# Stick-breaking attention: the scores of a head pair made in one go, in turns on two row groups and into two PSUM banks

## The chip, the cores and the metric

One NeuronCore of a Trainium2 chip runs the whole program; the other cores are idle. The metric is the device time of one execution in microseconds (us). TensorE (PE) does the matrix products, ScalarE (ACT) and VectorE (DVE) the elementwise work and the reading of PSUM, GpSimd (POOL) a few memsets and small operations, and SyncE (SP) issues the transfers. Each engine works through its own list of instructions strictly in the order in which the program was built.

## What is computed

A block of a streaming encoder over 528 tokens of width 1024: a feed-forward layer, a mixer with two kinds of attention, and a second feed-forward layer. The part that the change touches is the stick-breaking attention with 8 heads of width 64:

```
z = einsum('bhtd,bhsd->bhts', q, k) * scale
strict = s < t
log_1m = where(strict, log_sigmoid(-z), 0)
csum = cumsum(log_1m, axis=-1)
log_a = log_sigmoid(z) + csum[..., -1:] - csum
a = where(strict, exp(log_a), 0)
out = einsum('bhts,bhsd->bhtd', a, v)
```

So each score needs the sum of `log_1m` over all later keys. The kernel gets that sum as a product with a triangular matrix, key block by key block from the last to the first, and carries the sum of the later blocks in one row.

## The kernel before, in words

All float32 operands are split into a high and a low part (`split`: one cast and one subtraction), and a product is three matmuls: high by high, high by low, low by high (`mm3`).

The mixer's second part works on four **pairs** of heads, p = 0 to 3. For a pair, `sb_qk` makes the keys `KS` and queries `QS`: head 0 lies on partitions 0 to 63 of these tiles, head 1 on partitions 64 to 127. `sb_attn` then goes over five key blocks i = 4 to 0, which have 20, 146, 274, 400 and 512 query columns, and calls `sb_tile` for head 0 and then for head 1. One call of `sb_tile` is this chain, in which every link needs the one before it:

1. three score matmuls with 64 contraction rows into one PSUM tile `z` (line 1146);
2. DVE adds the mask (1150); ACT takes Abs, Exp and Ln (1154 to 1156); DVE adds max(z, 0) (1157), casts the result to `shi` (196) and subtracts for `slo` (197);
3. row 0 of `shi` and `slo` gets the carry, which is read from row 0 of the `z` tile of the previous key block of the same head (ACT 1164, DVE 1165);
4. two matmuls with the triangular matrix `tri` add the suffix sums onto `z` (1170 for `shi`, 1172 for `slo`);
5. ACT takes Exp (1175) and casts (192), DVE subtracts (197);
6. two matmuls with V add to the head's output `ysb` (1110, 1111). After the last block `out_v` copies and adds (1115, 1116).

A `z` tile is a whole PSUM bank; there are four of them (`bufs=4`), so two heads and two key blocks fill them. A head's `z` of one block is free once the carry of its next block has been read.

Between the steps of this chain PE works on other products, the **fillers**: `fillers()` makes the next pair's `QS` and `KS` (tiles pk, pq), the latents of the other attention (pc, pkr), the gates (`gt`, 24 matmuls of 512 columns for each), and the first parts of the latent attention (muqr, muqs, muk, muq, muv). How many of these are handed out between two tiles is set by `FILL_RATE`. The order of instructions on each engine is not written by hand: a scheduler builds it from the program, the priorities (`ATT_PRIO` for the stick-breaking tiles) and its own estimate of durations. Behind the fourth pair come the output projection `osb` (which needs all four pairs) and the latent attention (sc, pt, ymla).

Of the kernel before, what the change touches and what calls it, by code (L numbers as in the profile page):

```python
# [9 lines left out]
F32 = mybir.dt.float32  # L10
F32R = mybir.dt.float32r
AF = mybir.ActivationFunctionType
ALU = mybir.AluOpType
# [24 lines left out]
CST = [0, 112, 238, 366, 492]  # L38
KROWS = [128, 128, 128, 128, 21]
# [18 lines left out]
ATT_PRIO = 3000  # L58
# [25 lines left out]
class Block:  # L84
# [1033 lines left out]
    def sb_attn(self, qk, V, p):  # L1118
        yo = []
        prev = [None, None]  # L1120
        for i in range(4, -1, -1):
            for heads in ((0,), (1,)):
                with self.tc.high_priority(ATT_PRIO):
                    self.sb_tile(qk, V, p, i, heads, prev, yo)
                yield i == 0 and heads == (1,)
        with self.tc.high_priority(ATT_PRIO):
            t = self.M(f"ysb{p}")
            for h in range(2):
                self.out_v(t[64 * h:64 * h + 64, :512], yo[h], True)
        self.ysb = t  # L1130

    def sb_tile(self, qk, V, p, i, heads, prev, yo):
        nc, tc = self.nc, self.tc
        KS, QS = qk
        m, c0 = KROWS[i], CST[i]
        n = 512 - c0
        nh = len(heads)

        def three(t):
            return t[:m, :nh * n].rearrange("p (h c) -> p h c", h=nh)  # L1140
        pv = three(self.z("z"))
        for x, h in enumerate(heads):
            r = slice(64 * h, 64 * h + 64)
            kc = slice(128 * i, 128 * i + m)
            for t, (kx, qx) in enumerate(((0, 0), (0, 1), (1, 0))):
                nc.tensor.matmul(pv[:, x], KS[r, kx, kc], QS[r, qx, c0:512], start=x == 0 and t == 0, stop=False,
                                 skip_group_check=True)
        mw = MASKW[i]
        msl = self.ms[:m, SHIFT[i]:SHIFT[i] + mw]
        nc.vector.tensor_tensor(pv[:, :, :mw], pv[:, :, :mw],  # L1150
                                msl.unsqueeze(1).to_broadcast([m, nh, mw]), ALU.add)
        ev, hi, lo = three(self.E("e", F32)), three(self.E("shi")), three(self.E("slo"))
        with tc.issue_after(self.pre):
            nc.scalar.activation(ev, pv, AF.Abs)
            nc.scalar.activation(ev, ev, AF.Exp, scale=-1.0)
            nc.scalar.activation(ev, ev, AF.Ln, bias=1.0)
        nc.vector.scalar_tensor_tensor(ev, pv, 0.0, ev, ALU.max, ALU.add)
        self.split(hi, lo, ev, "dve")
        d = n
        if prev[heads[0]] is not None:  # L1160
            d = CST[i + 1] - c0
            pps, x = prev[heads[0]]
            src = pps[0:1, x:x + 1]
            nc.scalar.mul(hi[0:1, :, d:n], src, -1.0)
            nc.vector.scalar_tensor_tensor(lo[0:1, :, d:n], src, -1.0, hi[0:1, :, d:n].bitcast(F32),
                                           ALU.mult, ALU.subtract)
        nc.gpsimd.memset(hi[0:1, :, :d].bitcast(F32), 0.0)
        nc.gpsimd.memset(lo[0:1, :, :d].bitcast(F32), 0.0)
        for x in range(nh):
            nc.tensor.matmul(pv[:, x], self.tri[:m, :m], hi[:, x], start=False, stop=False,  # L1170
                             skip_group_check=True)
            nc.tensor.matmul(pv[:, x], self.tri[:m, :m], lo[:, x], start=False, stop=True,
                             skip_group_check=True)
        with tc.issue_after(self.pre):
            nc.scalar.activation(ev, pv, AF.Exp)
        self.split(hi, lo, ev, "act")
        if not yo:
            yo += [self.y("ysb") for _ in range(2)]
        for x, h in enumerate(heads):
            self.mm_v(yo[h], V[i], 2 * p + h, m, c0, hi[:, x], lo[:, x], i == 4, i == 0)  # L1180
            prev[h] = (pv, x)

    def mla_latents(self, a):

# [344 lines left out]
```

## Time and profile before

| | us |
|---|---|
| median of 3 runs (1213.14 to 1215.94) | 1213.72 |
| the profiled execution | 1213.73 |
| its span, first to last instruction | 1211.6 |
| PE busy in it | 1179.5 (97%) |
| ACT, DVE busy in it | 634.8, 833.1 |
| stick-breaking attention, first score to last V product | 431.7 to 672 |

The page gives busy times and the chain of work that ended last; the time line gives single instructions with their start and how long each took. Matmuls follow each other closely, so the pitch (start to start) says what a matmul costs, and its own duration is longer than that. A row of the time line with x3 stands for three instructions in a row; its second number is the time from the first start to the last end. What stands in brackets at the end of a row is how long the engine was idle before it and what ended the wait.

### The profile page before, as it was taken

What the parts mean: (1) busy time and instruction counts of PE and PEld (TensorE: products, weight loads), DVE (VectorE), ACT (ScalarE), POOL (GpSimd) and SP (SyncE); (2) the same over time, 40 slices, a digit from 0 to 9 for tenths busy, and PEclk for the clock granted to TensorE, in tenths of its full rate; (3) what the DMA queues carried; (4) which work ended last, traced back from release to release, by engine and by line L of the source; (5) the groups of instructions that cost most, each with busy time, mean ns of one, the idle gap of its engine ahead of it and who ended that gap; (6) DMA issues with size and microseconds to landing.
All of it is one profiled execution on the core that took longest, in us unless ns stands there. A gap on an engine that the chain in (4) does not pass through costs nothing.

```text
span 1211.6 us, 20678 instructions
## 1 busy us (share of the span) xinstructions
PE 1179.5 (97%) x7928; PEld 1067.2 (88%) x7928; DVE 833.1 (69%) x1628; ACT 634.8 (52%) x1353; POOL 114.4 (9%) x189
## 2 busy tenths in 40 slices
PE   8999999999999999999999999999999999999997
PEld 8999999999999977878876777768988999889987
DVE  7754886579778655655576667489785588458945
ACT  6544564245554446555666657556364466226632
POOL 0000000000000011110020333360000000000004
PEclk9999999999998999999999999999999999999999
DMA  6233234223431421223232135353144223313441
GB/s 217 71 101 91 90 104 140 71 87 98 166 122 55 149 96 62 88 87 106 83 106 84 62 101 178 103 185 123 36 161 154 70 90 125 118 54 105 148 148 70
DMA packets 46594, 130.29 MB, mean 108 GB/s; under 512 B 5368, under 2 KB 8824, under 8 KB 46496
## 3 DMA queue, kind: packets, MB, share of 16 engines
q1 hardware_dynamic: 46208, 128.88, 32.7%
q8 instruction: 62, 1.02, 0.3%
q14 instruction: 36, 0.29, 0.1%
q10 hardware_dynamic: 288, 0.10, 0.0%
HBM read 114.99 MB, written 12.58 MB: 105 GB/s over the span
## 4 chain that ended last, share of the span: by engine, by line
PE 86%; DVE 6%; ACT 3%; issue 2%; DMA 2%; POOL 1%; SPq 0%; DVEq 0%; ACTq 0%; POOLq 0%
PE pg L169 5%; PE pu L171 5%; PE pg L171 5%; PE pu L170 5%; PE pu L169 5%; PE pg L170 5%; PE down L732 3%; PE down L734 3%; PE down L733 3%; PE down L169 2%; PE down L171 2%; PE down L170 2%; PE gt L169 2%; PE gt L171 2%; PE gt L170 2%
## 5 line engine op out<-in xcount | busy, mean ns | idle before, releaser
L192 ACT CAST wp<-ws 128x512 fp32r<-128x512 f32 x144 | 87.1, 621 | 88.2 <-DVE ws L507 51.9
L197 DVE TENSOR_TENSOR wp<-ws,wp 128x512 fp32r<-128x512 f32 x144 | 97.0, 688 | 27.7 <-ACT wp L192 26.9
L197 DVE TENSOR_TENSOR wdl<-wdr,wdh 128x1024 fp32r<-128x1024 f32 (+1 forms) x42 | 49.2, 1172 | 42.7 <-ACT wdh L192 26.5
L192 ACT CAST wdh<-wdr 128x1024 fp32r<-128x1024 f32 (+1 forms) x42 | 42.4, 1009 | 56.4 <-PE pu L171 18.5
L169 PE MATMUL pu<-un,wp 128*128 128x264 f32 (+1 forms) x216 | 60.7, 283 | 0.0
L170 PE MATMUL pu<-un,wp 128*128 128x264 f32 (+1 forms) x216 | 60.7, 281 | 0.0
L170 PE MATMUL pg<-un,wp 128*128 128x264 f32 (+1 forms) x216 | 60.6, 282 | 0.0
L169 PE MATMUL pg<-un,wp 128*128 128x264 f32 (+1 forms) x216 | 60.5, 282 | 0.0
L171 PE MATMUL pu<-un,wp 128*128 128x264 f32 (+1 forms) x216 | 60.3, 282 | 0.0
L171 PE MATMUL pg<-un,wp 128*128 128x264 f32 (+1 forms) x216 | 60.2, 282 | 0.0
L169 PE MATMUL down<-g,wdh 128*128 128x272 f32 (+1 forms) x208 | 59.4, 290 | 0.4 <-ACT wdh L192 0.4
L170 PE MATMUL down<-g,wdh 128*128 128x272 f32 (+1 forms) x208 | 59.0, 287 | 0.0
L171 PE MATMUL down<-g,wdl 128*128 128x272 f32 (+1 forms) x208 | 58.8, 287 | 0.0
L733 PE MATMUL down<-wdl,g 128*128 128x512 f32 x144 | 56.8, 394 | 0.0
L734 PE MATMUL down<-wdh,g 128*128 128x512 f32 x144 | 56.1, 394 | 0.0
L732 PE MATMUL down<-wdh,g 128*128 128x512 f32 x144 | 55.1, 395 | 0.0
L169 PE MATMUL pg<-mcd,wp 128*128 128x264 f32 (+1 forms) x144 | 41.0, 285 | 1.7 <-ACT kept L497 1.7
L192 ACT CAST wp<-wpr 128x512 fp32r<-128x512 f32 x54 | 32.1, 621 | 18.9 <-DMA wpr<-g1p 11.2
L171 PE MATMUL pu<-mab,wp 128*128 128x264 f32 (+1 forms) x144 | 40.9, 284 | 0.0
L171 PE MATMUL pg<-mcd,wp 128*128 128x264 f32 (+1 forms) x144 | 40.9, 284 | 0.0
L170 PE MATMUL pg<-mcd,wp 128*128 128x264 f32 (+1 forms) x144 | 40.8, 283 | 0.0
L170 PE MATMUL pu<-mab,wp 128*128 128x264 f32 (+1 forms) x144 | 40.8, 283 | 0.0
(470 smaller groups left out, 4337.2 us busy)
## 6 DMA issues: line engine op xcount, KB each, us to landing
wdr<-d SPq DMA_DIRECT2D x38, 512.0 KB, 3.6
wpx<-u1p SPq DMA_DIRECT2D x18, 512.0 KB
wpr<-g1p SPq DMA_DIRECT2D x18, 512.0 KB, 3.7
wpx<-u2p SPq DMA_DIRECT2D x18, 512.0 KB, 4.7
wpr<-g2p SPq DMA_DIRECT2D x18, 512.0 KB, 3.8
wgtr<-w_in SPq DMA_DIRECT2D x16, 512.0 KB, 3.5
wxr<-w_out SPq DMA_DIRECT2D x8, 512.0 KB, 4.2
gl<-gates SPq DMA_DIRECT2D x16, 256.0 KB, 4.5
```

What stands on the lines that cost most here:

```text
L169: mm(out, wh, xh, start=first, stop=False, skip_group_check=True)
L170: mm(out, wh, xl, start=False, stop=False, skip_group_check=True)
L171: return mm(out, wl, xh, start=False, stop=last, skip_group_check=True).ins
L192: self.cast = nc.scalar.copy(hi, src).ins
L197: return nc.vector.tensor_tensor(lo, src, hi.bitcast(F32), ALU.subtract).ins
L732: mm(o, gt[:, 0, s], wh, start=fi == 0, stop=False, skip_group_check=True)
L733: mm(o, gt[:, 0, s], wl, start=False, stop=False, skip_group_check=True)
L734: mm(o, gt[:, 1, s], wh, start=False, stop=fi == nf - 1, skip_group_check=True)
```

## The change

The three score matmuls of a head leave `sb_tile`. A new function `sb_scores` takes two `z` tiles at once and issues the six score matmuls of both heads in turns: head 0, head 1, head 0, and so on, each ordered behind the one before it (`after(last)`). So neighbours read from partitions 0 to 63 and 64 to 127 and write to different banks. `sb_attn` calls it once per key block, and then `sb_tile` for each head with the tile that it is handed. The generality of `sb_tile` over several heads in one tile goes away with it; each tile still does the same elementwise work.

```diff
         for i in range(4, -1, -1):
-            for heads in ((0,), (1,)):
+            with self.tc.high_priority(ATT_PRIO):
+                pv = self.sb_scores(qk, i)
+            for h in range(2):
                 with self.tc.high_priority(ATT_PRIO):
-                    self.sb_tile(qk, V, p, i, heads, prev, yo)
-                yield i == 0 and heads == (1,)
+                    self.sb_tile(V, p, i, h, pv[h], prev, yo)
+                yield i == 0 and h == 1
...
+    def sb_scores(self, qk, i):
+
         KS, QS = qk
         m, c0 = KROWS[i], CST[i]
+        pv = [self.z("z")[:m, :512 - c0] for _ in range(2)]
+        kc = slice(128 * i, 128 * i + m)
+        last = None
+        for t, (kx, qx) in enumerate(((0, 0), (0, 1), (1, 0))):
+            for h in range(2):
+                r = slice(64 * h, 64 * h + 64)
+                with self.after(last):
+                    last = self.nc.tensor.matmul(pv[h], KS[r, kx, kc], QS[r, qx, c0:512], start=t == 0, stop=False,
+                                                 skip_group_check=True).ins
+        return pv
...
-        for x, h in enumerate(heads):
-            r = slice(64 * h, 64 * h + 64)
-            kc = slice(128 * i, 128 * i + m)
-            for t, (kx, qx) in enumerate(((0, 0), (0, 1), (1, 0))):
-                nc.tensor.matmul(pv[:, x], KS[r, kx, kc], QS[r, qx, c0:512], start=x == 0 and t == 0, stop=False,
-                                 skip_group_check=True)
```

The scheduler builds a new order from this. Three places show what it does. The names: z is a score tile, pv, gt, muk, muqr, muqs and muv are fillers, ysb are the products with V.

PE, first pair, the scores of 274 columns: two neighbouring pieces of the difference from before (-) to after (+).

```order
-L1170 MATMUL z<-shi,tri 128x146
-L1172 MATMUL z<-slo,tri 128x146
-L1146 MATMUL z<-QS_5158,KS_5094 128x274 x3
+L1172 MATMUL z<-shi,tri 128x146
+L1173 MATMUL z<-slo,tri 128x146
+L1145 MATMUL z<-QS_5158,KS_5094 128x274
 L170 MATMUL pv<-wvl,u_4552 128x512
 L171 MATMUL pv<-wvh,u_4552 128x512
```

```order
-L1170 MATMUL z<-shi,tri 128x146
-L1172 MATMUL z<-slo,tri 128x146
-L1146 MATMUL z<-QS_5158,KS_5094 128x274 x3
 L170 MATMUL pv<-wvl,u_4546 128x512
 L171 MATMUL pv<-wvh,u_4546 128x512
+L1172 MATMUL z<-shi,tri 128x146
+L1173 MATMUL z<-slo,tri 128x146
+L1145 MATMUL z<-QS_5158,KS_5094 128x274 x5
```

Two groups of three became a group of one (head 0 alone, as soon as its bank is free) and a group of five (once head 1's bank is free too); both heads' scores are whole at the end of the five.

PE, end of the third pair (p = 2): what follows the last scores, those of 512 columns. First before, from the products with `tri` of head 0 on:

```order
L1170 MATMUL z<-shi,tri 128x512
L169 MATMUL muqr<-ch,wuqrh 128x512
L1172 MATMUL z<-slo,tri 128x512
L1146 MATMUL z<-QS_6687,KS_6623 21x20 x3
L170 MATMUL muqr<-cl,wuqrh 128x512
L171 MATMUL muqr<-ch,wuqrl 128x512
L169 MATMUL muqs<-ch,wuqrh 128x512
L170 MATMUL muqs<-cl,wuqrh 128x512
L171 MATMUL muqs<-ch,wuqrl 128x512
L169 MATMUL muqs<-ch,wuqrh 128x512
```

And after, from the last products with V of 400 columns on:

```order
L1110 MATMUL ysb<-shi,V_5278 128x400
L1111 MATMUL ysb<-slo,V_5278 64x400
L1172 MATMUL z<-shi,tri 128x512
L1173 MATMUL z<-slo,tri 128x512
L1145 MATMUL z<-QS_6687,KS_6623 21x20 x6
L1110 MATMUL ysb<-shi,V_5246 128x512
L1172 MATMUL z<-shi,tri 128x512
L1111 MATMUL ysb<-slo,V_5246 64x512
L1173 MATMUL z<-slo,tri 128x512
L1145 MATMUL z<-QS_6687,KS_6623 128x146
L1172 MATMUL z<-shi,tri 21x20
L1173 MATMUL z<-slo,tri 21x20
```

Before, 59 fillers of 512 columns stand between head 1's scores and the pair's last product with V of 512 columns; after, only 8 fillers of 264 columns (muk) do, and the gate that filled the place stands behind them all. The ACT order at this place after the change, from head 0's Abs on:

```order
L1158 ACTIVATE e<-z 128x512
L192 CAST KM_7191<-muk 64x264
L1159 ACTIVATE e<-e 128x512
L1160 ACTIVATE e<-e 128x512
L1158 ACTIVATE e<-z 128x512
L1159 ACTIVATE e<-e 128x512
L1167 ACTIVATE shi<-z 1x400
L1160 ACTIVATE e<-e 128x512
L1175 ACTIVATE e<-z 128x512
L192 CAST shi<-e 128x512
L1167 ACTIVATE shi<-z 1x400
```

Abs, Exp and Ln of the two heads now stand one behind the other, since both heads' scores come at the same time.

PE, end of the fourth pair: what follows the last scores. Before, with head 1's last scores at the top:

```order
L1146 MATMUL z<-QS_6687,KS_6623 128x512 x3
L1172 MATMUL z<-slo,tri 128x400
L169 MATMUL muv<-wuvh,ch 16x512
L170 MATMUL muv<-wuvl,ch 16x512
L171 MATMUL muv<-wuvh,cl 16x512
L169 MATMUL gt<-u_4552,wgth 128x512
L1110 MATMUL ysb<-shi,V_5278 128x400
L170 MATMUL gt<-u_4552,wgth 128x512
L171 MATMUL gt<-u_4552,wgtl 128x512
L1111 MATMUL ysb<-slo,V_5278 64x400
```

After, with the group of five at the top:

```order
L1145 MATMUL z<-QS_6687,KS_6623 128x512 x5
L1173 MATMUL z<-slo,tri 128x400
L1111 MATMUL ysb<-slo,V_5278 64x400
L169 MATMUL muv<-wuvh,ch 128x512
L170 MATMUL muv<-wuvl,ch 128x512
L171 MATMUL muv<-wuvh,cl 128x512
L169 MATMUL muv<-wuvh,ch 128x512
L170 MATMUL muv<-wuvl,ch 128x512
L171 MATMUL muv<-wuvh,cl 128x512
L1110 MATMUL ysb<-shi,V_5278 128x400
L1111 MATMUL ysb<-slo,V_5278 64x400
L1172 MATMUL z<-shi,tri 128x512
```

From the last scores to the last product with V, 30 fillers of 512 columns (27 muv, 3 gt) stand before and 6 after; the 12 sc matmuls of the latent attention stand there in both. Over all four pairs, PE's runs of score matmuls with nothing else between them number 36 before and 39 after.

## Rows read from the trace of the kernel before

**Rows 1.** The page: the chain that ended last, by engine.

```profile
PE 86%; DVE 6%; ACT 3%; issue 2%; DMA 2%; POOL 1%; SPq 0%; DVEq 0%; ACTq 0%; POOLq 0%
```

**Rows 2.** Stretches: start:end, length, busy us (x instructions) of PE, PEld, DVE, ACT, POOL, clock, DMA.

```profile
600.00:625.00 25.00, 25.00 (x114) 18.52 (x113) 17.27 (x38) 16.33 (x37) 3.87 (x14) 1.00 0.33 111
...
650.00:675.00 25.00, 21.47 (x86) 15.15 (x84) 17.37 (x35) 18.07 (x38) 0.83 (x5) 0.93 0.26 74
...
700.00:800.00 100.00, 90.72 (x468) 69.92 (x466) 68.24 (x146) 65.39 (x153) 40.85 (x33) 0.98 0.43 144
```

**Rows 3.** Time line of PE: start, length, line, shape, count [idle before]. Scores among others.

```profile
474.90 0.49 PE L1146 MATMUL z<-QS,KS 64*128 64x512 f32 x1
475.33 0.34 PE L1111 MATMUL ysb<-slo,V 128*64 128x274 f32 x1
...
651.39 0.34 PE L1172 MATMUL z<-slo,tri 128*128 128x400 f32 x1
651.67 0.96 PE L1146 MATMUL z<-QS,KS 64*128 64x512 f32 x3
652.56 0.49 PE L171 MATMUL gt<-u,wgtl 128*128 128x512 f32 x1
652.89 0.39 PE L169 MATMUL gt<-u,wgth 128*128 128x512 f32 x1
653.12 0.40 PE L170 MATMUL gt<-u,wgth 128*128 128x512 f32 x1
```

**Rows 4.** Time line of PE: the two score matmuls in flight at 431.93.

```profile
431.78 0.31 PE L1146 MATMUL z<-QS,KS 64*128 64x146 f32 x2
```

**Rows 5.** Time line of PE: third pair, 512 columns, both heads' scores and last V product.

```profile
602.12 0.96 PE L1146 MATMUL z<-QS,KS 64*128 64x512 f32 x3
...
606.38 0.95 PE L1146 MATMUL z<-QS,KS 64*128 64x512 f32 x3
...
621.42 0.39 PE L1111 MATMUL ysb<-slo,V 128*64 128x512 f32 x1
```

**Rows 6.** Time line of ACT: links of the chain at 512 columns, fourth pair.

```profile
653.03 0.60 ACT L1154 ACTIVATE e<-z 128x512 f32<-128x512 f32 x1
...
654.32 0.63 ACT L1156 ACTIVATE e<-e 128x512 f32<-128x512 f32 x1
...
660.34 0.49 ACT L1164 ACTIVATE shi<-z 1x400 fp32r<-1x400 f32 x1
...
669.61 0.60 ACT L1175 ACTIVATE e<-z 128x512 f32<-128x512 f32 x1
670.30 0.62 ACT L192 CAST shi<-e 128x512 fp32r<-128x512 f32 x1
```

**Rows 7.** Time line of DVE: links of the chain at 512 columns, fourth pair.

```profile
654.98 0.69 DVE L1157 SCALAR_TENSOR_TENSOR e<-z,e 128x512 f32<-128x512 f32 x1 [1.42 <-ACT e L1156]
...
657.13 0.41 DVE L196 CAST shi<-e 128x512 fp32r<-128x512 f32 x1
...
661.61 0.56 DVE L1165 SCALAR_TENSOR_TENSOR slo<-z,shi 1x400 fp32r<-1x400 f32 x1
...
670.95 0.69 DVE L197 TENSOR_TENSOR slo<-e,shi 128x512 fp32r<-128x512 f32 x1 [0.79 <-ACT shi L192]
```

**Rows 8.** Time line of PE: end of the fourth pair.

```profile
656.83 0.45 PE L1172 MATMUL z<-slo,tri 128*128 128x400 f32 x1
...
660.97 0.47 PE L1170 MATMUL z<-shi,tri 128*128 128x512 f32 x1 [1.19 <-ACT shi L1164]
...
669.14 0.40 PE L1172 MATMUL z<-slo,tri 128*128 128x512 f32 x1
...
671.80 0.40 PE L1111 MATMUL ysb<-slo,V 128*64 128x512 f32 x1
```

**Rows 9.** Stretches, columns as in rows 2: just after that wait, and the whole end.

```profile
656.83:671.80 14.97, 13.60 (x56) 10.33 (x55) 10.40 (x21) 10.59 (x22) 0.63 (x4) 0.89 0.23 64
...
661.63:665.04 3.41, 3.41 (x11) 2.73 (x11) 2.15 (x6) 1.25 (x4) 0.00 (x0) 0.50 0.62 192
```

More of the change, by code (lines that the diff above doesn't have):

```diff
@@ L1130, in sb_attn, with sb_tile @@
         self.ysb = t
-    def sb_tile(self, qk, V, p, i, heads, prev, yo):
-        nc, tc = self.nc, self.tc
+    def sb_scores(self, qk, i):
         KS, QS = qk
         m, c0 = KROWS[i], CST[i]
-        n = 512 - c0
[L1137 to L1141, printed above, removed]
-        for x, h in enumerate(heads):
-            r = slice(64 * h, 64 * h + 64)
-            kc = slice(128 * i, 128 * i + m)
-            for t, (kx, qx) in enumerate(((0, 0), (0, 1), (1, 0))):
-                nc.tensor.matmul(pv[:, x], KS[r, kx, kc], QS[r, qx, c0:512], start=x == 0 and t == 0, stop=False,
-                                 skip_group_check=True)
+        pv = [self.z("z")[:m, :512 - c0] for _ in range(2)]
[8 more added lines that the diff above has]
+        return pv
+    def sb_tile(self, V, p, i, h, pv, prev, yo):
+        nc, tc = self.nc, self.tc
+        m, c0 = KROWS[i], CST[i]
+        n = 512 - c0
         mw = MASKW[i]
         msl = self.ms[:m, SHIFT[i]:SHIFT[i] + mw]
-        nc.vector.tensor_tensor(pv[:, :, :mw], pv[:, :, :mw],
-                                msl.unsqueeze(1).to_broadcast([m, nh, mw]), ALU.add)
-        ev, hi, lo = three(self.E("e", F32)), three(self.E("shi")), three(self.E("slo"))
+        nc.vector.tensor_tensor(pv[:, :mw], pv[:, :mw], msl, ALU.add)
+        ev, hi, lo = (t[:m, :n] for t in (self.E("e", F32), self.E("shi"), self.E("slo")))
         with tc.issue_after(self.pre):
@@ L1159, in sb_tile @@
         d = n
-        if prev[heads[0]] is not None:
+        if prev[h] is not None:
             d = CST[i + 1] - c0
[L1162 to L1165, printed above, removed]
+            src = prev[h][0:1]
+            nc.scalar.mul(hi[0:1, d:n], src, -1.0)
+            nc.vector.scalar_tensor_tensor(lo[0:1, d:n], src, -1.0, hi[0:1, d:n].bitcast(F32),
                                            ALU.mult, ALU.subtract)
[L1167 to L1173, printed above, removed]
+        nc.gpsimd.memset(hi[0:1, :d].bitcast(F32), 0.0)
+        nc.gpsimd.memset(lo[0:1, :d].bitcast(F32), 0.0)
+        nc.tensor.matmul(pv, self.tri[:m, :m], hi, start=False, stop=False, skip_group_check=True)
+        nc.tensor.matmul(pv, self.tri[:m, :m], lo, start=False, stop=True, skip_group_check=True)
         with tc.issue_after(self.pre):
@@ L1178, in sb_tile @@
             yo += [self.y("ysb") for _ in range(2)]
-        for x, h in enumerate(heads):
-            self.mm_v(yo[h], V[i], 2 * p + h, m, c0, hi[:, x], lo[:, x], i == 4, i == 0)
-            prev[h] = (pv, x)
+        self.mm_v(yo[h], V[i], 2 * p + h, m, c0, hi, lo, i == 4, i == 0)
+        prev[h] = pv
     def mla_latents(self, a):
```

## Prediction

> **What bounds the kernel now.** I read the chain that ended last first: TensorE holds 86% of it [rows 1]. So what counts is PE's work plus the time PE stands idle, stage by stage. Then the table of stretches: from 600 to 625 us, in the middle of the attention that is changed, PE is busy for all of 25.00 us, while ACT and DVE have room (16.33 and 17.27). From 650 to 675, where the fourth pair ends, PE is busy for 21.47 only, and from 700 to 800, in the latent attention, for 90.72 of 100 [rows 2]. So the stick-breaking stage is bound by PE's list as long as the list offers other work between the links of the attention chain. Saved PE time is then gained in full; a place where the list offers nothing is lost in full, since PE takes its instructions in order.
>
> **Part 1, the score matmuls.** The time line prices them by the pitch of starts. A gate matmul of 512 columns costs 0.23 (652.89 to 653.12). The triple of one head at 512 columns runs from 651.67 to 652.56, 0.89; with 0.28 ahead of it (0.18 would do for 400 columns) and 0.33 behind it (0.23 would do), a visit to the 64-row matmuls costs 0.10 + 0.20 + 0.10 = 0.40 over its columns. A single score matmul takes 0.43, 474.90 to 475.33 [rows 3].
>
> In a group of five, head 1's first stands beside head 0's second, and so on: three slots if neighbours on different rows run side by side. The trace holds such a case: in the first pair the scheduler happened to put two heads in turns, and two matmuls of 146 columns are in flight together, both within 0.31 [rows 4]; one behind the other, even at the pitch of a gate by columns, the second would start 0.07 later. At 146 columns a slot may be set by something other than the columns, so the row doesn't fix the gain at 512; I take the slots in full by it, and keep zero for the range. The Trainium skill (TensorE: Matmul & The Clock Gate, Part 3: Packing small matmuls) says that matmuls on different row groups run at the same time, starting about 4 ns apart, also at 512 columns; by it the slots come out in full.
>
> Before, a pair of triples has six slots; after, a group of one and a group of five have four. Two slots saved are 0.89 - 0.43 = 0.46 at 512 columns, by columns 0.36 at 400, 0.25 at 274 and 0.13 at 146. The first three occur in four pairs (4 x 1.07 = 4.28), the last in three, since the first pair's was in turns already (0.39): 4.7 us.
>
> Against it, the number of visits doesn't fall: because a group waits for head 1's bank, one visit of six became two, and some are cut further, 36 before and 39 after. Three more at 0.40 are 1.2. The Trainium skill (TensorEngine Tiling (Array Packing), Key Properties) says that changing the tiling mode drains the engine, which speaks against a change that cuts its groups; the 0.40 of the row agrees, and without that price the saving would be 4.7. **Saved on PE: 4.7 - 1.2 = 3.5 us** (bounds: +4.7 and -1.2).
>
> **Part 2, the third pair's end.** Both heads' scores are now whole at the same moment, so two chains run in step through ACT and DVE, and the scheduler put almost nothing between their links: 8 muk of 264 columns where 59 fillers of 512 stood. Before, both heads' scores of 512 columns ran at 602.12 and 606.38 and the last V product at 621.42, with PE never idle [rows 2, 5]. Now I lay the links one behind the other from the end of the group of five, with the durations of the fourth pair. ACT ends the 400-column tile of head 1 (Exp and cast, 0.60 and 0.62 by columns, about 1.0) and a muk cast (0.3); head 0's Abs, Exp and Ln take 1.92 (653.03 to 654.32, and 0.63): 3.2 [rows 6]. DVE's max-add 0.69 and cast 0.41, ACT's carry 0.49, DVE's carry 0.56 [rows 7]: 5.4. The product with `tri`, with its way to ACT of 0.47 (669.14 to 669.61) [rows 6, 8]: 5.9. Exp and cast, 0.60 and 0.62 with gaps, then head 1's carry 0.49: 7.7. DVE has head 0's subtraction (0.69) ahead of head 1's carry (0.56): about 8.4, and 8.9 after `tri`. Then head 1's Exp and cast, among small ones of the next pair (10.4), the subtraction 0.69, V 0.23 (11.4), and the 20-column products that the list puts ahead of the gate: **about 12 us**. PE's work in it: 8 muk at 0.12, four products of 400 columns at 0.18, eight of 512 at 0.23, and six small visits (20 and 146 columns) at about 0.4: 5.9. PE stands idle for 6.0. Bounds: 4 (ACT's operations at the closest pitch) and 7.5 (each link with a further wait). Before: 0.
>
> **Part 3, the fourth pair's end.** From the end of the last scores (656.83) to the last V product (671.80) the stage takes 14.97 before, of which PE is idle 1.19 in one wait for the carry [rows 8, 9]. The list moves work from behind the last scores to ahead of them: 24 fillers at 0.23 and one V product, 5.7. So the last scores come 5.7 later for this alone; behind them the two chains in step need about 12 us by the sum of part 2 (a weight cast of 1.0 on ACT in place of the 20-column work), against 14.97. The end of the attention moves by 5.7 - 3.0 = **+2.7** (bounds: +1.2 and +4.2, for a chain of 10.5 and 13.5).
>
> **Part 4, the clock.** After the wait of 1.19 the granted clock stood at 0.50 (1.2 GHz) from 661.63 to 665.04 [rows 9]. Such a stretch costs PE half of 3.41, 1.7, where PE has work. The long idle of part 2 should bring one more; part of it falls into the idle itself. I take 0.85 (bounds 0 and 1.7).
>
> **At no price:** the elementwise work is the same in number and size, and so are the transfers. The two loads of mask rows for the latent attention move behind a gate's store on SP; they are wanted after the attention. The rest of the list behind the attention is nearly the same, so a later end there is passed on one to one: the 9.3 us that PE idles from 700 to 800 [rows 2] are waits of the latent attention's own chain, which moves along. Elsewhere in the four pairs at least 6.6 us of PE work stand between a tile's scores and its `tri`, save two tiles of 20 columns, whose links are short, and I count nothing.
>
> **The sum**, against the profiled execution (1213.73, its span 1211.6 and 2.1 around it, within 0.01 of the median of 1213.72): -3.5 + 6.0 + 2.7 + 0.85 = +6.0. **1219.7 us**, slower by 0.5%. All bounds on their good side: -4.7 + 4 + 1.2 + 0 = +0.5; on their bad side, with the slots kept: -3.5 + 7.5 + 4.2 + 1.7 = +9.9.
>
> **Rivals.**
> - *Not slower: the two ends cost less than the links laid end to end.* ACT overlaps neighbours that don't depend on each other, as two heads' operations don't, so that the third pair's end idles for 4 us, the fourth's chain takes 10.5, no half-clock stretch is added and no visit is charged: +0.5, 1214.2. It decides the sign from the point where the two ends cost less than the slots give. For it: ACT was busy for only 16.33 of 25 us [rows 2]. Against it: the links within a head depend on each other, and 8 muk cover only one of some twelve microseconds. If moreover the half-clock stretch that is there at 661.63 falls into idle time, another 1.7 go: 1212.5, and a little more of each would make it faster than can be doubted.
> - *It doesn't do what it says:* the neighbours start together but share the columns' time. The 4.7 are gone: 1224.4. Against it, rows 4.
> - *Lockstep everywhere:* the group of five waits for head 1's bank, and the waiting PE holds the fillers behind it, at the other key blocks. At 0.3 each in seventeen blocks it is +5: 1224.8. Against it: before, PE doesn't wait at such places, and the list leaves 6.6 us or more.
>
> **Chances.** What the measurement can tell from no change is about 0.2%, 2.4 us: 1211.3 to 1216.1. The forecast (1216.5 to 1223.5) 0.60; the ends cost less 0.19, of which 0.14 within 0.2% and 0.05 faster; no side-by-side 0.12; lockstep 0.09. Slower: 0.60 + 0.12 + 0.09 = 0.81. The range takes in the first rival's centre and the two slow ones' but not their far halves: 1214.0 to 1225.0.
>
> **What would show it.** Part 1: in the time line, groups of five score matmuls of 512 columns that last about as long as the triples did (0.96), and starts in pairs; if they last 1.4, the second rival holds. Part 2: PE idle for some 6 us in the stretch of the third pair's last block, ended by ACT's carry and casts and DVE's subtractions, where it was busy throughout; if PE is busy there, the forecast is wrong. Part 3: from the last scores to the last V product about 12 us with half of it idle. Part 4: one more stretch at 0.50 near 610 to 625. Lockstep would show as waits of PE just before score matmuls of other blocks.

## The result and the profile after

The changed kernel takes **1231.19 us** (median of 4 runs, 1230.02 to 1236.02), the kernel before 1214.18 in the same comparison: ratio **1.0139** (1.0114 to 1.0165), slower by 17 us. The sign was forecast, the size was not: +6.0 was predicted, and the time lies above the range. The profiled execution of the changed kernel is the longest of its four (1236.02, span 1234.2), so I give times behind the attention with care.

The stretches of the changed kernel, columns as in [rows 2]:

```profile
600.00:625.00 25.00, 23.39 (x110) 17.81 (x108) 15.18 (x26) 15.80 (x30) 2.12 (x5) 1.00 0.35 112
625.00:650.00 25.00, 19.71 (x73) 13.67 (x74) 14.39 (x39) 12.79 (x39) 3.56 (x15) 0.66 0.07 18
650.00:675.00 25.00, 23.66 (x109) 17.44 (x106) 16.33 (x37) 17.43 (x39) 1.36 (x8) 1.00 0.28 90
675.00:700.00 25.00, 19.96 (x87) 15.15 (x86) 17.67 (x40) 16.72 (x41) 5.78 (x9) 0.86 0.20 55
700.00:800.00 100.00, 93.05 (x485) 72.36 (x485) 62.40 (x151) 61.12 (x151) 32.70 (x28) 0.97 0.35 114
```

Where PE had 114 matmuls in 25 us [rows 2], it now gets 73 done between 625 and 650, at a mean granted clock of 0.66. That is the third pair's end. PE's time line there:

```profile
620.52 0.96 PE L1145 MATMUL z<-QS,KS 64*128 64x512 f32 x5
621.41 0.39 PE L170 MATMUL muk<-cl,wukh 128*128 128x264 f32 x1
...
623.04 0.34 PE L1111 MATMUL ysb<-slo,V 128*64 128x400 f32 x1
627.21 0.76 PE L1172 MATMUL z<-shi,tri 128*128 128x512 f32 x1 [3.82 <-ACT shi L1167]
627.80 0.77 PE L1173 MATMUL z<-slo,tri 128*128 128x512 f32 x1
...
630.54 0.66 PE L1172 MATMUL z<-shi,tri 128*128 128x512 f32 x1
...
635.00 0.89 PE L1111 MATMUL ysb<-slo,V 128*64 128x512 f32 x2
637.30 0.38 PE L1110 MATMUL ysb<-shi,V 21*128 21x20 f32 x1 [1.41 <-DVE ysb L1116]
637.53 0.25 PE L1111 MATMUL ysb<-slo,V 21*64 21x20 f32 x1
638.11 0.80 PE L169 MATMUL gt<-u,wgth 128*128 128x512 f32 x1 [0.32 <-DVE KM L197]
```

The group of five lasts 0.89 (620.52 to 621.41), just as the triple of one head did [rows 3]. Then come the last eight muk and four V products, and PE waits. From the end of the last scores to the gate behind which PE works on without a wait 16.70 us pass. Links of that chain on ACT:

```profile
624.00 0.63 ACT L1160 ACTIVATE e<-e 128x512 f32<-128x512 f32 x1
...
626.57 0.49 ACT L1167 ACTIVATE shi<-z 1x400 fp32r<-1x400 f32 x1 [0.80 <-DVE slo L197]
...
628.61 0.60 ACT L1175 ACTIVATE e<-z 128x512 f32<-128x512 f32 x1 [1.02 <-PE z L1173]
...
632.39 0.65 ACT L1175 ACTIVATE e<-z 128x512 f32<-128x512 f32 x2
...
635.95 0.58 ACT L1115 COPY yl<-ysb 64x512 f32<-64x512 f32 x1
```

and on DVE:

```profile
624.66 0.69 DVE L1161 SCALAR_TENSOR_TENSOR e<-z,e 128x512 f32<-128x512 f32 x1 [0.77 <-ACT e L1160]
625.38 0.43 DVE L196 CAST shi<-e 128x512 fp32r<-128x512 f32 x1
625.85 0.69 DVE L197 TENSOR_TENSOR slo<-e,shi 128x512 fp32r<-128x512 f32 x1
627.10 0.56 DVE L1168 SCALAR_TENSOR_TENSOR slo<-z,shi 1x400 fp32r<-1x400 f32 x1 [0.56 <-ACT shi L1167]
...
636.56 0.68 DVE L1116 TENSOR_TENSOR ysb<-ysb,yl 64x512 f32<-64x512 f32 x1 [0.44 <-ACT yl L1115]
```

A row with x2 can hold two shapes: at 635.00 only the first of the two products has 512 columns, and it is the pair's last. The last two links (ACT 635.95, DVE 636.56) fold the third pair's `ysb` bank; the next pair's 20-column products with V want that bank, and PE waits for it at 637.30.

The fourth pair's end, PE:

```profile
676.16 0.39 PE L1111 MATMUL ysb<-slo,V 128*64 128x400 f32 x1 [0.16 <-DVE slo L197]
680.36 0.76 PE L1172 MATMUL z<-shi,tri 128*128 128x512 f32 x1 [3.81 <-ACT shi L1167]
...
687.86 0.45 PE L1111 MATMUL ysb<-slo,V 128*64 128x512 f32 x1 [0.23 <-DVE slo L197]
```

And the stretches that go with these places: third pair's chain, the half-clock stretch in it, what of that lies behind the gate, the fourth pair's end, and its half-clock stretch.

```profile
621.41:638.11 16.70, 9.80 (x42) 6.03 (x41) 12.57 (x33) 12.13 (x35) 1.73 (x9) 0.62 0.22 66
625.35:642.41 17.06, 12.12 (x38) 7.91 (x39) 11.77 (x33) 9.01 (x30) 3.56 (x15) 0.50 0.10 26
638.11:642.41 4.30, 4.30 (x10) 3.47 (x11) 2.05 (x8) 0.57 (x3) 1.83 (x6) 0.50 0.14 33
673.36:687.86 14.50, 9.79 (x30) 6.72 (x29) 9.71 (x19) 9.72 (x19) 0.63 (x4) 0.76 0.19 48
679.96:686.79 6.83, 6.08 (x17) 4.68 (x18) 4.59 (x9) 4.06 (x9) 0.51 (x4) 0.50 0.03 12
```

To see where the 17 us arise, I compare when the same amount of PE work is done in two executions: all matmuls counted by their columns (without the twenty that r_clock adds), the difference set to zero at 430 us, where the attention starts. Marks are on the clock of the kernel before. A mark inside the attention is good to about 1 us (r_rate70's at 650 to about 2), since the lists differ there; at 750 us all of the attention is done. The last two columns are the measured ratio of all runs and the number of PE's matmuls that stand elsewhere, by the two lists, from the out-projection of the mixer to the end. That number depends on what is counted as the same matmul; read from it only none, some (63 to 101) and many (194 to 271).

| kernel | 615 | 650 | 680 | 750 | 900 | ratio (95%) | moved behind |
|---|---|---|---|---|---|---|---|
| changed | -2.1 | +9.0 | +12.4 | +14.3 | +21.1 | 1.0139 (1.0114 to 1.0165) | 206 |
| r_heads | +0.4 | +0.2 | +0.3 | +0.2 | +3.4 | 1.0016 (0.9997 to 1.0035) | 271 |
| r_oldend | +0.2 | +4.2 | +7.1 | +7.7 | +15.0 | 1.0092 (1.0075 to 1.0109) | 206 |
| r_rate70 | +0.8 | +0.4 | +16.4 | +16.5 | +17.4 | 1.0099 (1.0082 to 1.0115) | 271 |
| r_clock | -3.6 | +7.2 | +10.7 | +12.7 | +18.4 | 1.0133 (1.0116 to 1.0150) | 194 |
| r_third | -3.6 | +7.1 | +4.5 | +9.5 | +12.4 | 1.0126 (1.0095 to 1.0158) | 206 |
| r_fourth | -0.3 | +0.1 | +3.9 | +4.1 | +3.4 | 1.0045 (1.0024 to 1.0065) | 63 |
| r_first2 | -1.7 | -1.7 | -3.2 | -4.8 | -1.8 | 1.0012 (0.9995 to 1.0029) | 271 |
| r_first2b | -2.8 | -2.8 | -5.3 | -4.8 | -1.4 | 0.9970 (0.9956 to 0.9984) | 97 |
| r_first1b | -1.4 | -1.4 | -3.8 | -3.3 | -2.1 | 0.9967 (0.9952 to 0.9983) | 101 |
| r_first2c | 0.0 | -0.2 | -0.1 | -0.2 | +1.5 | 0.9995 (0.9978 to 1.0012) | 63 |
| r_plain62 | 0.0 | 0.0 | -3.9 | -4.0 | -4.2 | 0.9978 (0.9964 to 0.9991) | 0 |
| r_change62 | -2.7 | +7.9 | +11.6 | +13.5 | +20.5 | 1.0131 (1.0113 to 1.0148) | 206 |

So against a lead of 2.1 at 615, the third pair's end loses 11.1 (615 to 650), the fourth's 3.4 (650 to 680), and 1.9 more go by 750: 14.3 in all. That is one execution for each kernel.

### The profile page after: what moved, and what is told of

Read it like the earlier page. It is cut to its first block, busy times and chain, and to the rows that moved or that the text cites. A ratio compares the mean times of both kernels' runs of the same rounds, so it can differ in the third digit from the quotient of the medians.

```text
span 1234.2 us, 20675 instructions
## 1 busy us (share of the span) xinstructions
PE 1188.8 (96%) x7928; PEld 1071.0 (87%) x7928; DVE 835.0 (68%) x1628; ACT 634.6 (51%) x1353; POOL 114.6 (9%) x189
## 5 line engine op out<-in xcount | busy, mean ns | idle before, releaser
L197 DVE TENSOR_TENSOR slo<-e,shi 128x146 fp32r<-128x146 f32 (+4 forms) x80 | 35.6, 446 | 25.9 <-ACT shi L192 22.9
L169 PE MATMUL pg<-mcd,wp 128*128 128x264 f32 (+1 forms) x144 | 41.5, 288 | 2.4 <-ACT kept L497 2.4
L171 PE MATMUL pg<-mab,wp 128*128 128x264 f32 (+1 forms) x144 | 40.9, 284 | 0.0
L171 PE MATMUL pg<-mcd,wp 128*128 128x264 f32 (+1 forms) x144 | 40.9, 284 | 0.0
L171 PE MATMUL pu<-mcd,wp 128*128 128x264 f32 (+1 forms) x144 | 40.8, 283 | 0.0
```

Source lines behind the costliest of these rows:

```text
L169: mm(out, wh, xh, start=first, stop=False, skip_group_check=True)
L171: return mm(out, wl, xh, start=False, stop=last, skip_group_check=True).ins
L197: return nc.vector.tensor_tensor(lo, src, hi.bitcast(F32), ALU.subtract).ins
```

## The experiments

**Theory A**, after the result: the slots are saved as forecast, and the loss is made where the list offers PE nothing while two heads' chains run (the ends of the third and fourth pair), by the length of that chain. Rivals: B, claiming two banks at once makes waits; C, two chains in step cost by themselves; D against A's part on the clock, E and F on where the loss sits. Later came G (a changed list behind the attention costs time there), H (that stage only scatters) and I (the constant `FILL_RATE` makes the gain).

### Both heads together, but not in turns (r_heads)

```diff
-        for t, (kx, qx) in enumerate(((0, 0), (0, 1), (1, 0))):
-            for h in range(2):
-                r = slice(64 * h, 64 * h + 64)
+        for h in range(2):
+            r = slice(64 * h, 64 * h + 64)
+            for t, (kx, qx) in enumerate(((0, 0), (0, 1), (1, 0))):
```

> Both heads' banks are claimed together and the six score matmuls stand behind one another as in the change, but head 0's three come ahead of head 1's three, so no two run on different rows. Theory A (the loss comes from the missing cover behind the groups of five, at the ends of the third and fourth pair): the list falls back almost to that of before, with gate matmuls behind each triple, so the time falls back with it: 1214 us, between 1212 and 1216. Rival B (claiming both banks at once makes PE or the chains wait): it stays at 1225 or more, and the slots that the turns saved (3.5 to 4.7 us) come on top: 1231 to 1236.

Measured: 1218.86 against 1216.32 for before on that chip, ratio 1.0016 with an interval that holds 1. The whole attention is within 0.4 us of before at every mark. So claiming both banks costs nothing, B falls, and the loss comes with the turns: with head 0's triple complete first, the scheduler comes back nearly to the list of before.

### The last key block head by head (r_oldend)

```diff
+            turns = i > 0
             with self.tc.high_priority(ATT_PRIO):
-                pv = self.sb_scores(qk, i)
+                pv = self.sb_scores(qk, i) if turns else None
             for h in range(2):
                 with self.tc.high_priority(ATT_PRIO):
-                    self.sb_tile(V, p, i, h, pv[h], prev, yo)
+                    sc = pv[h] if turns else self.sb_score(qk, i, h)
+                    self.sb_tile(V, p, i, h, sc, prev, yo)
```

(`sb_score` makes one head's three score matmuls. The next kernels with turns in some places only have the same edit with another condition.)

> The scores of the last key block of each pair (512 columns) are made head by head as before, all other blocks in turns. The list then has 7.2 us of work behind head 1's triple of the third pair, but again only 6 to 8 muk matmuls from head 0's first product with tri to the last V product. Theory A (missing cover): the loss at the third pair's end falls from 11.4 us to 3 to 5, that at the fourth stays at 3 to 5, and the lead by slots shrinks from 3.7 to about 2: 1217 to 1223 us. Rival C (two chains in step through ACT and DVE are the loss by themselves, cover or not): with the heads apart again the whole loss goes, 1211 to 1214. Rival B (groups of five cost more than they save): under 1 us better than the change, 1230.

Measured: 1.0092, 11 us above before, where A gave 3 to 9 and C gave 0 or less. The third pair's end loses 4.0 (from 615 to 650) where the change loses 11.1, the fourth 2.9. From its last scores to the gate the chain takes 14.58 us, with much more of it covered:

```profile
618.13:632.71 14.58, 12.19 (x61) 8.80 (x61) 12.51 (x28) 11.43 (x27) 3.00 (x8) 1.00 0.28 93
```

The heads are apart and there is still a loss, so C does not hold by itself; what shrank with the loss is the uncovered part. A's figures were a little low, mostly by what is lost behind the attention (7 us in the profiled execution).

### More fillers per tile (r_rate70)

```diff
-FILL_RATE = 0.65
+FILL_RATE = 0.70
```

> The changed kernel with one constant moved: 0.70 in place of 0.65 filler steps for each tile. The list then holds 7.7 us of gate and latent query matmuls between the group of five and the first product with tri at the third pair's end, and 4.4 us behind it, in place of eight muk; in the fourth pair the fillers run out earlier. Theory A: no wait of 3.8 us and no long stretch at half clock at the third pair's end; of the 11.4 us lost there over 8 are gone by 645 us; the fourth pair, with less left to lie under its links, loses more than before: 1219 to 1228 us in all. Rival C (two chains in step are slow by themselves): the last V product of the third pair still comes 16 us after the group of five and PE still loses over 8 us there: 1230 or more.

Measured: 1.0099. The third pair's end loses nothing that can be told (+0.8 at 615, +0.4 at 650) where it lost 11.1, with both heads still in step there; the fourth pair loses about 16 instead of 3.4. The stretches from the last scores of the third pair to the gate, and at half clock in the fourth:

```profile
623.10:644.74 21.64, 19.56 (x93) 14.47 (x93) 13.12 (x29) 13.57 (x30) 2.26 (x8) 1.00 0.25 80
664.13:688.03 23.90, 17.41 (x43) 10.37 (x43) 13.94 (x29) 13.50 (x28) 1.31 (x8) 0.50 0.12 30
```

The chain at the third end is even longer (21.64 us), and it costs nothing, since PE has 93 matmuls in it and its clock stays at 1.00. This is the clearest run against C. It also shows that the cover is a fixed stock: the fillers used at the third end are missing at the fourth. The total came out at the upper end of what A gave (by the medians 13 us, 5 to 14 expected).

### Filling the gap with matmuls that nobody reads (r_clock)

```diff
+    def keep(self, n):
+        for _ in range(n):
+            self.nc.tensor.matmul(self.zlast[1][:, 400:512], self.ones, self.ones[:, :112], start=True, stop=True,
+                                  skip_group_check=True)
...
+        if p in (2,) and i == 0 and h == 0:
+            self.keep(20)
         nc.gpsimd.memset(hi[0:1, :d].bitcast(F32), 0.0)
```

(`zlast[1]` is head 1's bank of the preceding key block. Line numbers in its rows are its own.)

> The changed kernel with twenty more matmuls (fp32, 112 columns of ones into unused columns of the preceding key block's bank, nothing reads them) between the group of five of the third pair and its first product with tri; the rest of the list stays. They do no useful work; PE should be busy with them for about 3.7 us of the wait of some 5. Theory A, its part on the clock: the granted clock falls because PE stands idle in that gap; with the gap filled the stretch of 17 us at 0.50 is gone or much shorter, and since PE was busy for 12.1 of these 17 us at half speed, 3 to 6 us come back: 1225 to 1228 us. Rival D (the chain of ACT and DVE sets the pace, the clock only stretches work that has time): 1229 to 1232, whatever the clock. If the twenty get in the way of V products: up to 1235.

Measured: 1.0133, no better than the change (1.0139). PE's time line and the stretches (last scores to gate; half clock):

```profile
619.56 1.71 PE L1152 MATMUL z<-ones 128*128 128x112 f32 x14
...
622.14 2.38 PE L1152 MATMUL z<-ones 128*128 128x112 f32 x20
624.29 0.48 PE L1180 MATMUL z<-shi,tri 128*128 128x512 f32 x1
```

```profile
618.12:634.42 16.30, 12.92 (x82) 9.84 (x81) 12.57 (x33) 12.13 (x35) 1.74 (x9) 0.83 0.23 68
628.89:639.13 10.24, 8.12 (x26) 5.85 (x25) 6.18 (x20) 4.51 (x18) 2.79 (x9) 0.50 0.16 42
```

Each of the twenty shows as two rows. The wait of 3.82 is gone, PE works without a gap up to the first product with `tri`, and that product still comes 6.17 us behind the last scores (5.80 in the change). From the last scores to the gate it takes 16.30 against 16.70. The half-clock stretch shrinks from 17.06 to 10.24 and starts 10.8 us behind the last scores instead of 3.9, and next to nothing is gained: the chain through ACT and DVE sets the pace (rival D). From the first product with `tri` to the gate the full clock gave back 0.8 us (10.13 against 10.90); 0.4 of it went to the twenty, which hold that product up. What the clock does cost at this place is the piece behind the gate, 4.30 us at half clock in the change (by half, about 2.15), 4.71 here.

### The third pair without the fourth, and the fourth without the third (r_third, r_fourth)

Conditions for turns: `p < 3`, and `p < 1 or p == 3`.

> Turns in the first three pairs, the fourth pair head by head as before. The list at the third pair's end is that of the change (eight muk and the two heads in step, none behind); the fourth's has 7.1 us of other work behind its last scores, where the change has 2.9. Theory A: the third end loses 11 to 12 us as in the change, the fourth 0 to 3 instead of 4.6, the lead by slots before that is 3 to 4: 8 to 11 us above before. Theory C' (each end loses the same few microseconds whatever stands there): 5 us at most at the third end, 2 to 4 above before. Rival F (most of the change's loss comes behind the attention, from the late start of what follows): within 3 us of the change, 14 above before or more.

> Turns in the first and the fourth pair only. The third pair's end keeps its 6.5 and 7.5 us of other work, the fourth pair's end has 2.9 us in place of 8.5 between its last scores and its last V product. Theory A (cover): nothing is lost at the third end; at the fourth the 5.6 us of work that moved ahead of the last scores are given back only where the chain behind them gets shorter than 15 us: PE idles 3 to 5 us more there, with a stretch or two at half clock; less 2 us of slots it comes out 1 to 5 us above before. Theory E (the fourth end loses only because the third end shifted everything): no loss there, 1 to 2 us below before.

Measured: 1.0126 and 1.0045. From the last scores of the third pair to the gate, first with the third pair in turns, then head by head with its cover; then the fourth pair's end of r_fourth:

```profile
620.93:638.52 17.59, 11.64 (x46) 7.56 (x45) 13.80 (x39) 12.96 (x39) 2.92 (x13) 0.70 0.16 53
```

```profile
607.87:626.35 18.48, 18.48 (x86) 14.00 (x86) 12.86 (x27) 10.38 (x23) 4.53 (x12) 1.00 0.32 107
664.93:679.42 14.49, 9.43 (x30) 6.40 (x29) 9.71 (x19) 9.72 (x19) 0.63 (x4) 0.76 0.20 48
```

The same stretch in the kernel before, from head 1's last scores to just behind its last V product:

```profile
607.27:625.68 18.41, 18.41 (x87) 14.00 (x86) 13.83 (x32) 11.74 (x30) 3.95 (x12) 1.00 0.33 108
```

The chains are about equally long in the three kernels (17.59, 18.48 and 18.41); in the first PE has 11.64 us of work at a mean clock of 0.70, in the other two it is busy throughout. So the change made the chain no longer; it took away what lay over it. Loss at the third end: 10.7 in r_third and 0.4 in r_fourth. At the fourth pair's end r_fourth loses 3.8 and r_third gains 2.6, so the fourth end loses on its own and rival E falls. At each end the kernel that has turns there loses what the change loses there. The totals do not add up so: 1.26% and 0.45% against 1.39%, and both lie above what A gave (8 to 11 and 1 to 5 us). r_third loses 5 us more by 750, most of it at 740, where a half-clock stretch of 6.83 stands; that I do not explain. F's figure for r_third's total came true (16 us by the medians), but not its reason: of the 13.5 us that its profiled execution is slower, 9.5 are there before 750.

### Turns only where cover stays (r_first2, r_first2b, r_first1b, r_first2c)

Conditions: `p < 1 or (p == 1 and i > 0)` (r_first2, and with `FILL_RATE = 0.62` r_first2b); `p == 0 or (p == 1 and i > 1)` with 0.62 (r_first1b); `p < 2 and i > 0` with 0.68 (r_first2c).

> Turns only in the first pair and in the key blocks of 400 columns and fewer of the second; everything else head by head as before. The list keeps at the third and the fourth pair's end just the work that stood there before (6.5 and 7.2 us of it at the third, 1.4 and 7.1 at the fourth), and at the first and second pair's ends there is 5 us or more ahead of the first product with tri. Theory A (the slots are real, and only ends without cover cost): the slots of six blocks, 0.46 + 2 x 0.36 + 2 x 0.25 + 0.13 = 1.8 us, less 0.8 if two or three more visits cost 0.4 each, stay to the end: 0.8 to 2 us below the kernel before, with no stretch at half clock near 620 to 645. Theory C (two chains in step cost by themselves, cover or not): each of the seven blocks in turns costs some tenths to a microsecond, and the time is 1 to 5 us above before.

> The same turns as in the run with turns only in the first pair and most of the second, with 0.62 filler steps for each tile in place of 0.65. The third and fourth pairs' ends keep the work that stood there before; what differs from that run is the list behind the mixer: 97 matmuls of the output projection and of the second FFN stand elsewhere than in the kernel before, where it was 271. Theory A with G (the lead of the slots, 1.7 us in that run, is real, and it was lost again behind the attention because the list there came out differently): 1 to 2 us below before. Rival H (what was lost behind the attention is the run to run scatter of that stage, whatever its list): within 1 us of the run it is compared with, 1 to 2 above before.

> As that, with turns in the first pair and in the key blocks of 274, 146 and 20 columns of the second alone, at 0.62: visits to the 64-row matmuls as many as before (35 and 35 by the list), slots 0.46 + 0.36 + 2 x 0.25 + 0.13 = 1.45 us, 101 matmuls elsewhere behind the mixer. Theory A with G: 1 to 2 us below before. Rival H: 0 to 2 above.

> Turns in the first two pairs without their last key blocks, 0.68 filler steps; the third pair's end keeps 4.9 and 7.5 us of other work, the fourth's 1.4 and 7.1; slots 2 x 0.36 + 2 x 0.25 + 0.13 = 1.35 us, three visits more; only 63 matmuls stand elsewhere behind the mixer, as few as in the run with turns in the first and fourth pair, which lost nothing there. Theory A with G: 0.5 to 1.5 us below before. Rival H: 0 to 2 above.

Measured: 1.0012, 0.9970, 0.9967 and 0.9995. In r_first2 the lead stands at 1.7 from 590 to 655 us, as the slots gave it (1.8), and no wait is added; yet the total, for which A gave 0.8 to 2 below before, shows none of it. In the profiled execution 3 us go again between 750 and 900, where 271 matmuls stand elsewhere in the list. With 97 and 101 moved, r_first2b and r_first1b are faster than before, by 0.3% and with intervals that end below 1; that is more than the 1 to 2 us that A with G gave. r_first2c, whose lead was gone by 615, comes out equal, where A with G gave 0.5 to 1.5 below. But the constant was moved in these three as well:

### The constant alone (r_plain62), and with the change (r_change62)

The kernel before, and the changed one, each with `FILL_RATE = 0.62`.

> The kernel before with 0.62 filler steps for each tile and no turns at all: the control for the two runs that came out 0.3% faster. Its list behind the mixer is that of the kernel before, and so is the work at the third and fourth pairs' ends. Theory A with G (the gain of those runs is the turns'): 1214, within 0.1% of before. Rival I (the constant made the gain): 1210 to 1211.

> The changed kernel, all four pairs in turns, with 0.62. The third pair's end again has nothing but muk matmuls (1.3 us) between its last scores and its last V product, the fourth's 2.9 us. Theory A with G: as slow as the change at 0.65, 14 to 18 us above before. Rival I (the constant decides): within 5 us of before.

Measured: 0.9978 (0.9964 to 0.9991) and 1.0131. So the constant alone gives 0.2%, which I had not expected: rival I holds for most of that gain. It arises in one place. The stretch round the fourth pair's end, before and r_plain62:

```profile
655.00:685.00 30.00, 26.39 (x115) 20.28 (x114) 19.29 (x45) 19.30 (x46) 5.76 (x9) 0.89 0.20 59
```

```profile
655.00:685.00 30.00, 26.98 (x136) 20.63 (x135) 21.83 (x49) 21.84 (x52) 5.76 (x9) 1.00 0.26 75
```

With 0.62 the list has the second product with `tri` of the 400-column block ahead of head 1's last score matmuls instead of behind them, and six more muv ahead of head 1's own product with `tri`; the wait of 1.19 [rows 8] is gone, both half-clock stretches (661.63 and 675.28, 3.41 each) with it, and PE gets 136 matmuls done in place of 115: 3.9 us. r_first2b and r_first1b gain 2.5 and 2.4 at the same place. What the turns add to it (1.4 and 2.8 us at 650) is not separated from the constant by the totals: 0.9970 and 0.9967 against 0.9978, intervals overlapping. The changed kernel with 0.62 is as slow as with 0.65, so the move to 0.62 does not decide about the change.

## Why the prediction was right in sign and wrong in size

- **What bounds the kernel: right.** A gap in PE's list is paid in full. With two heads in step at the third pair's end, the chain costs nothing with 93 matmuls in it (r_rate70) and 11.1 us with 42.
- **Part 1 (-3.5): right.** A group of five takes 0.89, as the triple did; starts in pairs. The kernels in turns that have no half-clock stretch ahead of it (r_clock, r_third) lead by 3.6 at 615 us; the slots of the blocks up to there are 3.0. So the slots come out in full, and the charge for more visits does not show. The rival "doesn't do what it says" falls. The Trainium skill's page TensorE: Matmul & The Clock Gate (Part 3: Packing small matmuls) is borne out at 512 columns: in the single starts of the trace, neighbours on different rows begin 3 or 4 ns apart (one pair 9), where it says about 4.
- **Part 2 (+6.0, the third pair's end): the step that failed, in size.** It measured 11.1. The mechanism, the place and the missing cover were right; the length of the chain was not. The sum ended at "about 12 us", and the gate came at 16.70, which is 4.7 of the 5.1 that the term was short.
  - Of the 4.7, 2.2 were lost by the last V product (13.6 instead of 11.4). They begin in the first half of the sum, which went from the cast straight to ACT's carry: the carry overwrites row 0 of `shi`, so it waited for DVE's subtraction, which reads it (0.69 at 625.85; the wait stands at 626.57). So DVE's carry of head 0 ended 6.25 behind the last scores, not 5.4. Then the second product with `tri` came 0.60 behind the first, and ACT's Exp of head 0 began at 7.2 instead of 5.9; by head 1's Exp (632.39) the delay was 2.1, 11.0 instead of 8.9. The half clock has little to do with it: r_clock, at full clock up to 628.89, has its last V product at 13.2 (631.30). In the waits of before, from 425 to 680, ACT's wait for the subtraction is plain (us in all, times, longest):

```profile
ACT shi L1164 <- DVE slo L197: 12.7, 12, 1.8
```

  - The other 2.5 I left out: I put the 20-column products ahead of the gate at almost nothing, but they want the `ysb` bank that the third pair's result must first leave by a copy on ACT (0.58) and an add on DVE (0.68). That bank's wait can be read from the names in the list, but no row of before shows it, since the cover hid it there.
  - The chain of 16.70 less PE's work in it, priced at 5.9, is 10.8, about what was lost. That PE's idle time alone came near the forecast (16.70 - 9.80 = 6.9, against 6.0) is luck: the chain was longer, and the work was shown busy for 9.80, mostly at half clock.
- **A row misread, without harm.** [rows 5] and the forecast take 621.42 for the third pair's last V product. That is head 0's; head 1's comes at 625.45. PE is busy up to there too, so "Before: 0" holds.

```profile
625.45 0.40 PE L1111 MATMUL ysb<-slo,V 128*64 128x512 f32 x1
```

- **Part 3 (+2.7, the fourth pair's end): sign and total about right, its parts wrong.** It measured 3.4 to 3.8 (650 to 680 in the change, r_clock, r_fourth, r_change62). I let the chain shorten from 14.97 to 12; it took 14.50, so the saving of 3.0 was 0.5, which makes +5.2. By the last V product the trace indeed shows more than 6 lost (6.5 in the change, 6.6 in r_fourth). About 3 of them come back by 680, where the kernel before waits 1.43 and 0.81 and has its half-clock stretch of 675.28, and the changed one has 0.23 of waits and full clock. That was not foreseen, so the nearness of the total is luck. The rows of before, the waits and then the stretch:

```profile
673.63 0.39 PE L169 MATMUL sc<-KM,QM 100*128 100x272 f32 x1 [1.43 <-ACT prob L1427]
...
675.08 0.43 PE L169 MATMUL muk<-ch,wukh 128*128 128x264 f32 x1 [0.81 <-DVE mV L197]
675.28:678.69 3.41, 3.41 (x16) 3.24 (x16) 1.99 (x6) 1.25 (x5) 1.14 (x2) 0.50 0.35 122
```

- **Part 4 (+0.85, the clock): too small, though less than the stretch looks.** One stretch of 17.06 us in place of the 3.4 that I had in mind, but r_clock shows that most of it is hidden in the chain. What it costs is the piece behind the gate, at most 2.15 (inside the 11.1 above). Another 1.9 come behind the attention, where the stretch at 717 lasts 6.83 instead of 3.41, and a stretch at 529.77 costs 1.5: r_clock, with the same list there, has none and leads by 3.6 at 615, not 2.1.
- **"Nothing elsewhere" in the attention: right.** Up to the third pair's end PE waits at no group of five; there the next pair's groups of 20 and 146 columns wait 0.55 and 0.38. So the rival of lockstep everywhere falls. That ends cost less falls too.
- **"The rest is passed on one to one": wrong by about 3 us.** At 750 the loss is 14.3, by the medians 17.0. I judged the list behind the attention to be nearly the same; 206 matmuls of the out-projection and the second FFN stand elsewhere. Kernels with a changed list there lose 1 to 7 us between 750 and 900 in their profiled executions, with two exceptions (r_rate70 +0.9, r_fourth -0.7), and r_heads, whose attention is that of before, loses 3. The only one with the old list, r_plain62, loses none. That the list is the cause was not tested by itself and stays open.

## What to carry to other kernels

A saving on the busiest engine is real only as long as the list keeps work behind the instructions that got faster: count, at each place, the other work that the new list holds between a chain's first and last link, before and after, and take the full length of the chain, less PE's own work in it, as the price where it holds none. Lay that chain link by link, with what an engine waits for before it may overwrite a row, to the first instruction that runs on freely, and look for buffers that must be emptied on the way (here a PSUM bank that the next pair wants). Turns are worth having only where the cover survives; and a stock of fillers moved to one gap is missing at the next.

## What the runs showed of the hardware

- In the change the half-clock stretch (1.2 GHz) of the third pair's end lasts 17.06 us, with PE shown busy for 12.12 of them; through its last 4.30 PE works on gates without a gap. In r_rate70 one lasts 23.90 with 17.41 busy. [rows 9] has one of 3.41. Just ahead of the long one in the change PE had been waiting since 623.4. In r_clock it had no wait up to 625.3, and the clock still fell, at 628.89, after a few short products with waits of 0.69 and 0.46 between them.
- A stretch of 3.41 us at half clock that PE works through cost 1.5 us: r_first2's lead steps from 1.7 to 3.2 between 660 and 665, where before has the stretch of [rows 9] and r_first2 has none.
- Two score matmuls of 512 columns on rows 0 to 63 and 64 to 127 into two banks run fully side by side: a group of five takes 0.89, as three of one head did.
